# Gate projections placed behind head pairs in the first attention, and key halves copied by VectorE in the second

## The chip, the cores and the metric

One Trainium2 chip, one core. The metric is the device time of the whole kernel in microseconds (us), the median of three timed runs. Engines are named as in the profile: PE (TensorE matmuls), PEld (its weight loads), ACT (ScalarE), DVE (VectorE), POOL (GpSimd), SP (SyncE, which issues most transfers).

## What is computed

Two transformer blocks in a row on 512 tokens of width 1024, in float32. The parts that the change touches, shortened:

```python
# first block: window attention over latent and context keys, 16 query heads, 4 key heads
att_lat = window_ctx_attention(q_l, k_l, v_l, k_c, v_c, sink)
out_lat = merge_branches(p_lat, ssd_lat, att_lat, w_o_ssd, w_o_att, w_out)

def merge_branches(p, y_ssd, y_att, w_o_ssd, w_o_att, w_out):
    gates = jax.nn.sigmoid(p[..., G0:D_IN])
    g_ssd, g_att = gates[..., :D_MODEL], gates[..., D_MODEL:]
    return (g_ssd * (y_ssd @ w_o_ssd) + g_att * (y_att @ w_o_att)) @ w_out

# second block: forgetting attention, 12 heads of 64, one key head for each
s = jnp.einsum('bhqd,bhkd->bhqk', qi, kh)
s = s + Fi[..., None] - F[:, :, None, :]
s = jnp.where(key_pos[None, :] <= qpos[:, None], s, NEG)
p = jax.nn.softmax(s, axis=-1)
return jnp.einsum('bhqk,bhkd->bhqd', p, vh)
```

Around them stand a state-space branch (SSD), a feed-forward network with a convolution, an S5 branch, an attention over a memory, and the projections of all of them.

## The kernel before

All operands lie feature-major: 128 features on the partitions, 512 tokens along the free dimension. A projection multiplies eight 128x128 weight blocks with eight activation tiles. To keep float32 accuracy each operand is held as a rounded part (`hi`) and a remainder (`lo`), and `mm3` (L220) makes three matmuls of 128x512 for each block: hi x hi (L221), hi x lo (L222), lo x hi (L223). So a projection is 24 such matmuls.

`load_w` (L212) brings one block row of weights: an SP transfer of 512 KB into `raw` (3 buffers), the rounding `whi` on ACT (L181 through the helper `act`), the remainder `wlo` on DVE (L184 through the helper `tt`). `whi` and `wlo` have two buffers each, so two sets of weights can be ready at a time.

The order of each engine's instructions is made when the program is built. A planner goes through the instructions with a simulated clock and puts each on its engine's queue by priority, which is the order of the program text unless `tc.high_priority` raises it; a tile gets a buffer when one of its tag is free. `tc.issue_after(ins)` makes the instructions traced inside it, those on the engine of `ins`, stand behind `ins` in that engine's queue. On the chip each queue then runs in its fixed order, with semaphores between engines.

First attention (L714 to L921): eight head pairs i = 0 to 7, each 128 features of queries. `att_q(i)` (L831) projects the queries (two banks of PSUM for projections, `set_banks(2)`, L717), copies them to `u` (one buffer, shared with the gates' `tg`), rotates them (`roped`, partly on POOL) and splits them into `qq` (two buffers). `att(i)` (L839) works on two half pairs, the query blocks (0, 1) and (3, 2): for each head the scores (L852 to L856), row maxima on DVE (L782), exponentials on ACT, the scaling on DVE (L797), transposes on PE (L807, tile `pT`) and their copies on ACT (`pt`), and at the end of the half the product with the values (L872, tile `y`, 36 matmuls). The results go to `yaa` (pairs 0 to 3) and `yab` (pairs 4 to 7).

Work that does not hang on the attention is written between the pairs. `gate_ssd(m)` (L893), m = 0 to 7, projects one block of the SSD gates, takes a tanh (`tg`) and multiplies it into `p1`. `half_proj` (L881, tile `po`) multiplies `yaa` with half of `w_o_att`: each of its four steps needs all four tiles of `yaa` for two output blocks. `mod_steps(4, ...)` makes a modulation vector. In the text, gates stand behind the pairs by a list (L905): behind pair 1 gate 0, behind pair 2 gate 1, and so on, gates 5 and 6 behind pair 6, gate 7 behind pair 7; `half_proj` and `mod_steps` advance one step behind each of the pairs 4 to 7.

Second attention (L1560 to L1614): six head pairs, then four heads of the memory attention. `fox_in(i)` (L1560) projects the keys to `kk`, rounds them to `kh` and takes the remainder `kl`, then does the same with the queries. `fox(i)` (L1576) makes scores from `kh`, `kl`, `qq` and `lh` (L1590 to L1592; `lh` is partly cast on POOL, L1583), then the same chain of row maxima, exponentials, transposes and value products. `fox_in` of the next pair is written ahead of `fox` of this one. For head j of a pair, the rounded keys `kh[:, j]` fill all 128 partitions: the 64 of the head itself and a second copy in the other 64. Before, ACT makes both from `kk` (L1569), four 64x512 instructions for each pair.

Of the kernel before, what the change touches and what calls it, by code (L numbers as in the profile page):

```python
# [156 lines left out]
def emit(ctx, tc, A, out):  # L157
# [681 lines left out]
    def att(i):  # L839
# [4 lines left out]
        def score(n, hh):  # L844
# [11 lines left out]
                    T.matmul(sc[:, pos[j]:pos[j] + P], lhsT=identb, rhs=m_, start=False, stop=x == len(mk) - 1)  # L856
            return sc[:, rng[0]:rng[1]]

        for ns in ((0, 1), (3, 2)):
            pts = {}  # L860
            for hh in range(2):
                pr = softmax_rows([lambda n=n: score(n, hh) for n in ns], col("sink", 2 * i + hh), qp, 640, 4)
                for x, n in enumerate(ns):
                    nb = 5 if n in (1, 2) else 4
                    pts[n, hh] = transposed([pr[x][:, c * P:(c + 1) * P] for c in range(nb)], qp, 5, 4)

            with tc.high_priority(offset=1000):
                for n in ns[::-1]:
                    kbs = [0, 1] + [2 + j for j in (n - 1, n, n + 1) if 0 <= j < 4]
                    for x, kb in reversed(list(enumerate(kbs))):  # L870
                        for hh in (1, 0):
                            mm = T.matmul(py[64 * hh:64 * hh + 64, n * P:(n + 1) * P],  # L872
                                          lhsT=vx[:, kb, kv * 64:kv * 64 + 64], rhs=pts[n, hh][:, x],
                                          start=(x == len(kbs) - 1), stop=(x == 0)).ins
                            in_order(mm, first=(n == ns[1] and x == len(kbs) - 1 and hh == 1))
        ya = yaa if i < 4 else yab
        done = act(ya[:, 0, i % 4], py, AF.Copy)
        tt(ya[:, 1, i % 4], py, f(ya[:, 0, i % 4]), SUB)
        return done

    def half_proj(w, ya, consume):  # L881

# [19 lines left out]
    att_q(0)  # L902
    first = half_proj(A["w_oa"][0], yaa, lambda m, po: act(p2[:, m], po, AF.Copy))
    mod4 = mod_steps(4, mod_raw(4))
    fill = {1: [0], 2: [1], 3: [2], 4: [3], 5: [4], 6: [5, 6], 7: [7]}  # L905
    for i in range(8):
        if i < 7:
            att_q(i + 1)
        done = att(i)
        if i == 1:  # L910
            with tc.issue_after(done.ins):
                act(s5ls, s5ls, AF.Exp)
        for m in fill.get(i, []):
            gate_ssd(m)
        if i >= 4:
            next(first)
            next(mod4)
# [642 lines left out]
    def fox_in(i):  # L1560
# [4 lines left out]
        kl = kls[i % 2]  # L1565
        for j in range(2):
            src = kk[64 * j:64 * j + 64]
            for q0 in (0, 64):
                act(kh[q0:q0 + 64, j], src, AF.Copy)  # L1569
            tt(kl[64 * j:64 * j + 64, j], src, f(kh[64 * j:64 * j + 64, j]), SUB)  # L1570
        a = proj2(U_Q + i)
        r = rtile("r")
        act(r, a, AF.Copy, scale=0.125)
# [256 lines left out]
```

## Time and profile before

| what | us |
|---|---|
| median of three timed runs | 2050.18 |
| the three runs | 2053.67, 2044.92, 2050.18 |
| the profiled execution: its time | 2044.51 |
| the profiled execution: its span | 2042.7 |
| PE busy | 1967.9 (96%) |
| DVE busy | 1349.4 (66%) |
| ACT busy | 966.5 (47%) |

The span is the time from the first to the last instruction of the profiled execution; its own time is 1.8 us longer. Busy time of PE counts each matmul with its modelled latency, so that 96% doesn't mean that PE works at its peak, but a stretch in which its busy time is less than the stretch's length has idle time for certain. The granted clock is the share of TensorE's full clock in a stretch; 1.00 is 2.4 GHz, 0.50 is 1.2 GHz.

### The profile page before, as it was taken

The page shows a single profiled execution, that of the slowest core. Times are in us where ns is not written, and L with a number is a line of the kernel's source. Part 1 is how long each engine was busy: PE and PEld are TensorE (multiplying, and loading weights), DVE is VectorE, ACT ScalarE, POOL GpSimd, SP SyncE. Part 2 cuts the span into 40 slices and gives each one's busy share as a digit, 9 for nine tenths or more (in the row PEclk, how much of TensorE's full clock was granted, in tenths as well). Part 3 has the DMA queues.
Part 4 walks back from the last instruction along what each step waited for, and adds up shares of the span by engine and source line. Part 5 has one row for each costly group of instructions (what it writes and reads, how often), then busy time and mean ns, then how long its engine had stood idle before and what let it go on. Part 6 is the DMA issues. An engine that isn't in the chain of part 4 may idle for free.

```text
span 2042.7 us, 29489 instructions
## 1 busy us (share of the span) xinstructions
PE 1967.9 (96%) x11312; PEld 1614.0 (79%) x11312; DVE 1349.4 (66%) x2376; ACT 966.5 (47%) x1825; POOL 215.3 (11%) x358
## 2 busy tenths in 40 slices
PE   6998999999999899999999999999999899999998
PEld 4787888788888777778777778878988677888887
DVE  6878877878657775457988886673587655524344
ACT  6745554454235665435443244454465544423233
POOL 2111101101030000001001110001432100000000
PEclk9998999999999999999999999999999999999999
DMA  7444545545312023333354643335764112333332
GB/s 296 116 126 131 158 134 174 165 148 162 111 55 70 22 73 94 104 124 110 120 170 124 217 147 97 100 117 170 203 169 121 51 61 59 132 96 89 102 96 90
DMA packets 84667, 250.48 MB, mean 123 GB/s; under 512 B 11632, under 2 KB 23280, under 8 KB 83760
## 3 DMA queue, kind: packets, MB, share of 16 engines
q1 hardware_dynamic: 67376, 199.45, 31.4%
q0 software_dynamic: 17152, 49.17, 7.8%
q8 instruction: 89, 1.46, 0.3%
q14 instruction: 50, 0.41, 0.1%
HBM read 228.78 MB, written 16.65 MB: 120 GB/s over the span
## 4 chain that ended last, share of the span: by engine, by line
PE 81%; DVE 7%; issue 6%; ACT 3%; DMA 2%; POOL 1%; SPq 0%; DVEq 0%; ACTq 0%; POOLq 0%
PE p L221 6%; PE p L222 6%; PE p L223 6%; PE pl L221 5%; PE pl L223 5%; PE pl L222 5%; PE pT L807 2%; PE po L221 2%; PE po L223 2%; PE po L222 2%; PE ub L223 2%; PE ua L223 2%; PE ub L221 2%; PE ub L222 2%; PE ua L221 2%
## 5 line engine op out<-in xcount | busy, mean ns | idle before, releaser
L184 DVE TENSOR_TENSOR wlo<-raw,whi 128x1024 fp32r<-128x1024 f32 (+3 forms) x283 | 329.0, 1164 | 297.4 <-ACT whi L181 287.1
L181 ACT ACTIVATE whi<-raw 128x1024 fp32r<-128x1024 f32 (+3 forms) x283 | 282.3, 999 | 441.0 <-PE p L222 139.1
L221 PE MATMUL pl<-hl,whi 128*128 128x512 f32 x528 | 212.2, 402 | 3.8 <-DVE cv L187 3.0
L223 PE MATMUL pl<-hl,wlo 128*128 128x512 f32 x528 | 209.5, 397 | 0.7 <-DVE wlo L184 0.7
L222 PE MATMUL pl<-hl,whi 128*128 128x512 f32 x528 | 209.6, 397 | 0.0
L221 PE MATMUL p<-h,whi 128*128 128x512 f32 x504 | 201.3, 401 | 1.9 <-ACT uf L181 0.8
L223 PE MATMUL p<-h,wlo 128*128 128x512 f32 x504 | 201.7, 401 | 1.1 <-DVE wlo L184 1.1
L222 PE MATMUL p<-h,whi 128*128 128x512 f32 x504 | 201.9, 401 | 0.0
L221 PEld LDWEIGHTS pl<-hl,whi 128*128 128x128 f32 x528 | 100.4, 190 | 23.6 <-DVE cv L187 3.2
L223 PEld LDWEIGHTS pl<-hl,wlo 128*128 128x128 f32 x528 | 100.1, 190 | 23.2 <-DVE wlo L184 2.4
L221 PEld LDWEIGHTS p<-h,whi 128*128 128x128 f32 x504 | 95.6, 190 | 25.0 <-ACT uf L181 1.2
L181 ACT ACTIVATE p<-s,nm 128x512 f32<-128x512 f32 (+4 forms) x128 | 80.1, 627 | 74.2 <-PE pT L807 35.0
L223 PEld LDWEIGHTS p<-h,wlo 128*128 128x128 f32 x504 | 95.5, 189 | 23.3 <-DVE wlo L184 2.0
L782 DVE TENSOR_REDUCE nm<-s 128x1 f32<-128x512 f32 (+4 forms) x128 | 76.7, 611 | 55.5 <-PE s L1592 29.9
L222 PEld LDWEIGHTS p<-h,whi 128*128 128x128 f32 x504 | 95.4, 189 | 21.9 <-DVE h L184 0.3
L222 PEld LDWEIGHTS pl<-hl,whi 128*128 128x128 f32 x528 | 100.4, 190 | 14.9
L181 ACT ACTIVATE inj<-cs_t,dwt 128x128 f32<-128x128 f32 x256 | 81.1, 391 | 45.0 <-DVE es L635 36.9
L181 ACT ACTIVATE pt<-pT 128x512 f32<-128x512 f32 (+1 forms) x152 | 70.6, 478 | 63.5 <-PE pT L807 52.9
L807 PE MATMUL pT<-cs_t,p 128*128 128x128 f32 x440 | 72.4, 278 | 9.9 <-ACT pt L181 9.6
L640 POOL DMA_DIRECT2D cf<-rows x64 | 34.7, 549 | 354.4 <-PE y L659 348.4
L223 PE MATMUL pdn<-uh,wlo 128*128 128x512 f32 x176 | 69.4, 395 | 1.0 <-DVE wlo L184 1.0
L223 PE MATMUL ua<-hf,wlo 128*128 128x512 f32 x176 | 69.4, 394 | 0.7 <-DVE wlo L184 0.7
(543 smaller groups left out, 4771.7 us busy)
## 6 DMA issues: line engine op xcount, KB each, us to landing
raw<-in_w_ta SPq DMA_DIRECT2D x66, 512.0 KB, 3.6
raw<-in_w_tb SPq DMA_DIRECT2D x63, 512.0 KB, 3.6
raw<-in_w_up SPq DMA_DIRECT2D x44, 512.0 KB, 3.7
es<-rows POOLq DMA_DIRECT2D x64, 256.0 KB, 5.8
cf<-rows POOLq DMA_DIRECT2D x64, 256.0 KB, 4.8
raw<-in_w_mod SPq DMA_DIRECT2D x32, 512.0 KB, 3.8
raw<-in_w_os SPq DMA_DIRECT2D x16, 512.0 KB, 4.1
raw<-in_w_out SPq DMA_DIRECT2D x16, 512.0 KB, 3.6
```

The costliest lines, as they stand in the source:

```text
L181: return S.activation(o, i, f, **kw)
L184: return eng.tensor_tensor(o, a, b, op=op)
L221: T.matmul(ps, lhsT=wh, rhs=ah, start=first, stop=False)
L222: T.matmul(ps, lhsT=wh, rhs=al, start=False, stop=False)
L223: T.matmul(ps, lhsT=wl, rhs=ah, start=False, stop=last)
L640: QS.dma_start(out=c_, in_=rows[r, 1].partition_broadcast(P))
L782: V.tensor_reduce(nm[:, j:j + 1], src, axis=AX.X, op=MAX)
L807: T.transpose(pt[:, j * P:(j + 1) * P], b, ident)
```

## The change

First attention: the list of gates is replaced. Each entry now has a half: a gate with half 1 is traced behind the last value product (`y`) of the first half of pair i, a gate with half 0 behind the last value product of pair i - 1. `att` returns these two instructions. The instruction given to `issue_after` is a matmul, so that the gates' matmuls are tied, and their transfers, roundings and products on other engines are not. Second attention: ACT rounds only the head's own half of the keys, and DVE copies that rounded half to the other 64 partitions.

```diff
+        mids = []
         for ns in ((0, 1), (3, 2)):
...
+            mids.append(mm)
...
-        return done
+        return done, mids
...
-    fill = {1: [0], 2: [1], 3: [2], 4: [3], 5: [4], 6: [5, 6], 7: [7]}
+
+    fill = {0: [(1, 0)], 1: [(1, 1)], 2: [(0, 2), (1, 3)], 3: [(0, 4), (1, 5)], 5: [(1, 6)], 7: [(0, 7)]}
+    last_y = None
     for i in range(8):
         if i < 7:
             att_q(i + 1)
-        done = att(i)
+        done, mids = att(i)
...
-        for m in fill.get(i, []):
-            gate_ssd(m)
+        for half, m in fill.get(i, []):
+            after_ = mids[0] if half else last_y
+            with tc.issue_after(after_):
+                gate_ssd(m)
+        last_y = mids[1]
...
         for j in range(2):
             src = kk[64 * j:64 * j + 64]
-            for q0 in (0, 64):
-                act(kh[q0:q0 + 64, j], src, AF.Copy)
-            tt(kl[64 * j:64 * j + 64, j], src, f(kh[64 * j:64 * j + 64, j]), SUB)
+            own, other = slice(64 * j, 64 * j + 64), slice(64 - 64 * j, 128 - 64 * j)
+            act(kh[own, j], src, AF.Copy)
+            V.tensor_copy(kh[other, j], f(kh[own, j]))
+            tt(kl[own, j], src, f(kh[own, j]), SUB)
```

## Rows read from the trace of the kernel before

**Rows 1.** The page, part 1: busy us, share of the span, instructions.

```profile
PE 1967.9 (96%) x11312; PEld 1614.0 (79%) x11312; DVE 1349.4 (66%) x2376; ACT 966.5 (47%) x1825; POOL 215.3 (11%) x358
```

**Rows 2.** Busy us by stretch: length, PE, PEld, DVE, ACT, POOL, clock, DMA share, GB/s.

```profile
613.00:661.20 48.20, 48.20 (x309) 39.39 (x309) 35.63 (x72) 28.87 (x59) 2.56 (x2) 1.00 0.24 73
661.20:685.00 23.80, 22.80 (x185) 18.66 (x185) 17.11 (x38) 16.45 (x38) 1.28 (x1) 1.00 0.15 46
685.00:704.40 19.40, 15.95 (x150) 12.66 (x148) 14.63 (x35) 13.71 (x35) 1.28 (x1) 1.00 0.01 2
704.40:724.00 19.60, 16.62 (x155) 13.04 (x155) 13.87 (x36) 13.62 (x35) 0.00 (x0) 1.00 0.00 1
...
724.00:823.30 99.30, 99.23 (x743) 78.84 (x742) 61.89 (x133) 59.00 (x132) 2.55 (x2) 1.00 0.30 91
...
823.30:838.80 15.50, 12.49 (x129) 10.26 (x129) 7.40 (x18) 9.49 (x22) 0.00 (x0) 1.00 0.11 35
```

**Rows 3.** The same for instructions on `pl`, the projections: PE, PEld, DVE, ACT.

```profile
613.00:661.20 48.20, 35.13 (x135) 24.25 (x134) 0.00 (x0) 2.92 (x5) 1.00 0.24 73
...
704.40:724.00 19.60, 0.00 (x0) 0.00 (x0) 0.00 (x0) 0.00 (x0) 1.00 0.00 1
```

**Rows 4.** PE in order of time, first attention: start us, us, engine, line, instruction.

```profile
673.70 0.50 PE L221 MATMUL pl<-hl,whi 128*128 128x512 f32 x1
...
679.68 0.48 PE L221 MATMUL po<-yaa,whi 128*128 128x512 f32 x1
...
727.46 0.40 PE L223 MATMUL po<-yaa,wlo 128*128 128x512 f32 x1
...
731.07 0.50 PE L221 MATMUL pl<-hl,whi 128*128 128x512 f32 x1
```

**Rows 5.** Groups by shape, 1480 to 1700 us, ACT and DVE: count, busy us, mean ns.

```profile
L181 ACT ACTIVATE whi<-raw 128x1024 fp32r<-128x1024 f32 x23 | 24.3, 1057 | 22.1 <-PE p L222 10.2 <-issue 8.5 <-PE pg L222 3.3
L181 ACT ACTIVATE kh<-kk 64x512 fp32r<-64x512 f32 x20 | 12.6, 628 | 1.1 <-PE s L1590 0.8
...
L184 DVE TENSOR_TENSOR wlo<-raw,whi 128x1024 fp32r<-128x1024 f32 x22 | 26.8, 1220 | 5.1 <-ACT whi L181 4.6 <-DMA w<-s5k 0.3
L184 DVE TENSOR_TENSOR qq<-r,qq 64x512 fp32r<-64x512 f32 x10 | 6.9, 686 | 1.1 <-ACT qq L181 0.8
```

**Rows 6.** Instructions of tiles `fhi` and `lh`: duration ns min/median/max, first and last start.

```profile
L1544 DVE CAST fhi<-fe x1: 428/428/428, 1422.4 to 1422.4; 128x512 fp32r<-128x512 f32 x1
...
L1583 POOL CAST lh<-qq x12: 611/846/1602, 1475.6 to 1652.4; 64x512 fp32r<-64x512 f32 x12
```

**Rows 7.** ACT in order of time, second attention: start us, us, instruction.

```profile
1586.68 2.55 ACT L181 ACTIVATE kh<-kk 64x512 fp32r<-64x512 f32 x4
1589.25 1.06 ACT L181 ACTIVATE whi<-raw 128x1024 fp32r<-128x1024 f32 x1
1590.21 0.26 ACT L181 ACTIVATE pt<-pT 128x128 f32<-128x128 f32 x1
```

**Rows 8.** PE in order of time; in brackets the idle time before, and who ended it.

```profile
1590.53 0.74 PE L807 MATMUL pT<-cs_t,p 128*128 128x128 f32 x4 [2.78 <-ACT pt L181]
...
1621.09 0.66 PE L807 MATMUL pT<-cs_t,p 128*128 128x128 f32 x4 [2.55 <-ACT pt L181]
...
1691.89 0.66 PE L807 MATMUL pT<-cs_t,p 128*128 128x128 f32 x4 [1.36 <-ACT pt L181]
```

**Rows 9.** Busy us by stretch of the second attention, columns as in rows 2.

```profile
1585.00:1592.00 7.00, 4.22 (x24) 2.96 (x22) 4.36 (x11) 6.20 (x15) 2.29 (x4) 0.93 0.19 25
1592.00:1616.00 24.00, 23.18 (x137) 18.62 (x137) 18.54 (x40) 13.66 (x30) 1.32 (x1) 0.95 0.21 61
1616.00:1623.00 7.00, 4.45 (x25) 3.17 (x24) 3.95 (x9) 6.64 (x16) 0.84 (x1) 0.91 0.00 0
1623.00:1640.00 17.00, 15.86 (x97) 12.94 (x99) 9.81 (x23) 6.76 (x15) 0.85 (x1) 0.94 0.24 66
1640.00:1705.00 65.00, 61.26 (x365) 48.64 (x361) 32.42 (x79) 27.46 (x67) 0.85 (x1) 1.00 0.21 67
```

## The prediction

> **What bounds the kernel now.** I read the page's busy shares first: TensorE (PE) is busy 96% of the span and no other engine passes 66% [rows 1]. So a change counts only if it takes away idle time of PE (or time at its lower clock); PE's own work is the same before and after. Then I looked for that idle time stage by stage.
>
> In the first attention the busy time by head pair [rows 2] shows where it lies (length minus PE busy): none in pair 0, 1.00 us in pair 1, 3.45 in pair 2, 2.98 in pair 3, 0.07 in pairs 4 to 6 together, 3.01 in pair 7. The matmuls of the projections alone [rows 3] say why: about 135 of them, over five projections of 24, run beside pair 0, and none beside pair 3. An attention pair needs scores, row maxima, exponentials, transposes, so PE waits for ScalarE (ACT) and VectorE (DVE) unless it has other matmuls. The order of PE in that stretch [rows 4] names the blocker: a gate projection (gate 3, by the tanh that follows) starts at 673.7, the next to take its place is `po` of `half_proj`, at 679.7, and its last part runs only at 727.5, because its k=3 needs head pair 3. There are two projection banks (`set_banks(2)`). Two `po` sit in both from about 700 on, and the next projection starts at 731.1. The gates 0 to 3 had been spent early, where PE was full anyway.
>
> In the second attention the ACT queue [rows 7] shows four `kh` copies, 2.55 us in a row, then a weight rounding, and behind them the small `pt` copy at 1590.21 that PE's next transposes wait for. PE's gap there is 2.78 us, and in the same place one pair later 2.55 us [rows 8]. Both have a second cost: the granted clock falls to its lower level (1.2 instead of 2.4 GHz) for a while after each. Summing length times missing clock over the four stretches [rows 9]: 7 x 0.07 + 24 x 0.05 + 7 x 0.09 + 17 x 0.06 = 3.3 us.
>
> **First attention, step by step.** Nothing is added or removed; eight `gate_ssd` move. Their PE instructions are queued behind the last `y` matmul of a half pair: gate 0 in the middle of pair 0, gate 1 in the middle of pair 1, gate 2 at the end of pair 1, gate 3 in the middle of pair 2, gate 4 at its end, gate 5 in the middle of pair 3, gate 6 in the middle of pair 5, gate 7 at the end of pair 6. A projection is under 6.0 us of PE, transposes between included (673.7 to 679.7 [rows 4]); a starved half pair lacks (3.45 + 2.98) / 4 = 1.6 us. So one projection per half fills it more than three times over; it costs PE nothing new, as the same matmuls are taken from pair 0. And the `po` of `half_proj` now comes after gate 5 in program order, so it gets its weights, and so a bank, only in pair 3.
> What goes: 1.00 + 3.45 + 2.98 = 7.4 us in pairs 1 to 3, and half of pair 7's 3.0 (gate 7 fills the first half only): together 8.9 us.
> What comes: (a) the first half of pair 0 has only query projection 2 beside it. It is at least a starved half, 1.6 us, and at most a starved pair doubled, 6.4 us; I take two starved halves, 3.2, since nothing of that half is begun beforehand. (b) The pin holds only PE instructions. The gates' loads, roundings (ACT) and remainders (DVE) still come early and keep one of the two `whi`/`wlo` pairs each until the gate has run. Behind the parked weights stand the next projection's rounding and remainder, 1.06 + 1.22 = 2.3 us [rows 5]. The first such handover, between projections 1 and 2, has little cover: 0 to 1.9 us, I take 0.5. (c) Later handovers lie beside attention work; bounds 0 and 4 us, I take 1.0, which is less than one starved half, in pair 6, whose second half may be left without a projection.
> What is hidden: the tanh, the `p1` products and their POOL multiply are the same instructions; p1 is next read after the stage, so their lateness costs nothing, unless gate 7's lands at the very end, where the next projections cover it. On SP the gates' weight loads change their turn with the others' (0.5 MB each); DMA share is at most 0.30 in every stretch here [rows 2], so I cost them at nothing.
> Sum: -8.9 + 3.2 + 0.5 + 1.0 = -4.2 us; bounds -7.3 and +3.4.
>
> **Second attention, step by step.** Off ACT: 12 copies of 64x512 at 0.628 us = 7.5 us [rows 5]. Onto DVE: 12 copies. The trace has no such copy across partition halves. The nearest rows are a rounding of 128x512 on DVE, 0.428 us [rows 6], and a subtraction of 64x512 that does cross, 0.686 [rows 5]; I take 0.43, as the copy too has one input, so 5.2 us in all, at most 8.2. In four of the six `fox_in` other work covers the ACT block, and its relief is worth nothing. In the two of [rows 8] the block shrinks by two copies, 1.26 us each. The gaps that are left, about 1.5 and 1.3 us, are like the 1.36 us gap at 1691.9 [rows 8], in a stretch whose clock stayed at 1.00 [rows 9]. I take it that the clock stays up here too, and the 3.3 us come back. That is 2.5 + 3.3 = 5.8 us if the queues keep their order. They are planned anew, so I count one event whole and the other half: 4.4 us. Bounds: 8.7 (both gaps and the clock: 2.78 + 2.55 + 3.3) and, below nothing, -1.7 (four added copies of 0.43 in front of a row maximum that PE waits for).
> The change adds one wait: the DVE copy waits for its own half's ACT rounding. Behind it on DVE stand the `kl` remainder, which waited for the same thing before, then row maxima and weight remainders, for which PE and ACT wait. ACT is then free 1.26 us sooner, so the wait is short.
>
> **A rule against it.** The casts of `lh` on POOL take 0.61 to 1.60 us, the same work each time [rows 6]. The Trainium skill (SBUF — State Buffer, section "SBUF: two separate sides") says that DVE and GpSimd share one port pair by an exclusive lock, which a DVE copy in a two-port mode holds for its whole length. By that rule the four copies near the two gaps could hold up the casts 1.7 us, and the second part would give 2.7 instead of 4.4, the whole 6.9.
>
> **Sum.** -4.2 - 4.4 = -8.6 us. The profiled run took 2044.51 us (span 2042.7 and 1.8 around it), so 2035.9, a ratio of 0.9958. The median of the three timed runs lies 5.7 us above the profiled run; on it the ratio gives 2041.5.
>
> **Rivals.** Forecast: about 2041.5, between 2036 and 2047 (0.38).
> Both in full: the order holds and the first half of pair 0 is only a starved half: -7.3 - 8.7 = -16.0, 2034 (0.20). For it: the gaps are few and have one cause each. Against: the plan is new.
> Nothing comes of it: the planner fills the first attention a half early or late and gives the 4 us back elsewhere, and a weight rounding of 1.06 us takes the place of the `kh` copies in front of `pt`: 2050 (0.20). For it: 1.06 us of `whi` already stands in that block [rows 7].
> The DVE copies cost: they go ahead of row maxima or hold up the `lh` casts; the second part gives 1 us or less, whole sum -5.2, 2045 (0.12).
> Slower: parked gate weights starve PE. Each parked gate leaves one weight pair to all other projections; where a handover's 2.3 us isn't covered, a half without a gap becomes a starved one. It decides when more than about six of the ten halves of pairs 0, 1, 4, 5, 6 lose their cover (6 x 1.6 = 9.6 against 8.9 won). With all ten, and one fall of the clock as after the long gaps (3.3 / 2 = 1.7): 10 x 1.6 + 1.7 - 8.9 = +8.8 us, 2059, more if the second part loses too (0.10).
>
> **Chances.** A measurement of this kernel tells about 0.5%, 10.3 us, from no change. Faster by more: all of the full case and under half of the forecast, 0.37. Slower by more: over half of the starving case, 0.06. Within: 0.57. The range takes in the forecast, the full case with 3 us of scatter and nothing at all: 2031 to 2055; left out are the starving case and some of the full one's lower end.
>
> **What would show it.** In the trace after: PE idle of pairs 2 and 3 under 1 us each, with a projection beside each half; `po` not before pair 3; a gap of 2 to 4 us in the first half of pair 0; two `kh` copies in a row on ACT instead of four; PE gaps near 1590 and 1620 at 1.5 us or less with the clock at 1.00. I am wrong if projections bunch again, if PE idles in pairs 4 to 6, or if the long gaps stay with something else ahead of `pt`.

## The result and the profile after

| | before | after |
|---|---|---|
| median, us | 2048.89 | 2084.51 |
| its runs, us | 2044.92 to 2053.67 | 2081.98 to 2088.30 |
| profiled execution: time, span | 2044.51, 2042.7 | 2081.98, 2080.2 |

The ratio of after to before is 1.0162, with a 95% interval of 1.0141 to 1.0183: the change makes the kernel slower, by about 33 us (the two medians lie 35.6 apart). The prediction was 2041.5, its range ended at 2055, and slower had a chance of 0.06.

Five stretches tell where the 37.5 us of the two spans lie. The marks between them are instructions that both kernels have: the last `kx` copy on ACT (the first attention begins), the last `y` copy of the first attention, the first `kh` copy, and the last score matmul on `kh`.

| stretch | before, us | after, us | more |
|---|---|---|---|
| up to the first attention | 588.6 | 591.3 | 2.7 |
| first attention | 250.2 | 277.8 | 27.6 |
| between the attentions | 627.9 | 631.0 | 3.1 |
| second attention | 220.8 | 224.6 | 3.8 |
| rest | 355.2 | 355.5 | 0.3 |

No edit of the change touches the stretch between the attentions. In the ten kernels of this study whose matmuls stand there in the very order of before (before among them) it took 627.9 to 634.5 us. So its 3.1 us are scatter, which a sum over one profiled execution doesn't see. The first attention took 250.0 to 251.8 us in each of the nine kernels without ties (before among them), so its 27.6 us are no scatter.

The page after, part 1, answers to [rows 1]. PE is busy 18 us longer with the same 11312 matmuls, which is already a hint of a lower clock:

```profile
PE 1986.0 (95%) x11312; PEld 1624.1 (78%) x11312; DVE 1352.7 (65%) x2388; ACT 959.1 (46%) x1813; POOL 214.7 (10%) x358
```

Busy us by head pair of the first attention after, columns as in [rows 2], to which it answers; the limits are the ends of the pairs:

```profile
591.30:650.70 59.40, 50.62 (x323) 41.26 (x322) 30.92 (x57) 26.98 (x55) 4.94 (x3) 0.91 0.15 45
650.70:683.30 32.60, 27.65 (x197) 22.93 (x197) 19.53 (x43) 16.86 (x39) 1.27 (x1) 0.90 0.11 33
683.30:721.30 38.00, 35.24 (x225) 29.03 (x226) 22.77 (x50) 19.75 (x46) 1.34 (x1) 0.91 0.18 56
721.30:756.70 35.40, 33.80 (x233) 27.43 (x231) 22.93 (x50) 19.57 (x44) 2.14 (x1) 1.00 0.15 46
756.70:784.70 28.00, 24.93 (x219) 18.61 (x219) 18.86 (x42) 17.39 (x40) 1.27 (x1) 1.00 0.38 122
784.70:817.50 32.80, 29.40 (x223) 23.03 (x224) 18.62 (x46) 19.10 (x47) 0.00 (x0) 1.00 0.13 42
817.50:845.40 27.90, 26.77 (x210) 20.93 (x211) 16.55 (x35) 16.60 (x38) 2.19 (x1) 1.00 0.31 95
845.40:869.10 23.70, 22.20 (x177) 18.53 (x174) 11.32 (x26) 13.07 (x29) 0.00 (x0) 1.00 0.16 46
```

Length minus PE busy is idle time: 8.8, 5.0, 2.8, 1.6, 3.1, 3.4, 1.1 and 1.5, together 27.2 us, where before had 10.9 within the same marks. And the clock, 1.00 in every stretch of [rows 2], is 0.91, 0.90 and 0.91 in the first three pairs: 59.4 x 0.09 + 32.6 x 0.10 + 38.0 x 0.09 = 12.0 us lost to it. 16.3 of idle and 12.0 of clock make 28.3, a little more than the 27.6 us: of the 23.8 us at the lower clock PE is idle for 5.5, and these count in both.

The projections' matmuls alone (tile `pl`: PE, PEld, DVE, ACT), in the two halves of pair 0 and the first of pair 1, which answers to [rows 3]:

```profile
613.00:634.00 21.00, 0.00 (x0) 0.00 (x0) 0.00 (x0) 0.00 (x0) 0.76 0.08 26
634.00:650.70 16.70, 12.03 (x48) 8.64 (x48) 0.00 (x0) 1.16 (x2) 1.00 0.11 33
650.70:667.20 16.50, 0.00 (x0) 0.00 (x0) 0.00 (x0) 0.00 (x0) 0.79 0.11 33
```

There is no projection at all beside the two first halves, two in the second half of pair 0. PE's waits in the first attention after (who waits, for whom, us in total, times, longest) say the same: it waits for exponentials, and hardly for the projections' weights. One wait of 2.4 us is for a transfer of the modulation's weights, in pair 4; before has no such wait.

```profile
PE s L852 <- ACT p L181: 17.0, 16, 4.8
...
PE mod L320 <- DMA raw<-in_w_mod: 2.4, 1, 2.4
...
PE pl L223 <- DVE wlo L184: 0.4, 1, 0.4
```

The next two fences show why that is not for want of weights. First ACT and DVE in order of time (start us, us, instruction): the weights of query projection 2 are rounded at 611.42, as soon as projection 1 has freed them, and their remainder is made at 612.51.

```profile
611.42 1.06 ACT L181 ACTIVATE whi<-raw 128x1024 fp32r<-128x1024 f32 x1
612.51 1.23 DVE L184 TENSOR_TENSOR wlo<-raw,whi 128x1024 fp32r<-128x1024 f32 x1 [0.33 <-ACT whi L181]
```

Then PE, which answers to [rows 4], and behind it on ACT the two evictions that tell whose projections these were (`tg` is a gate's, `u` a query's):

```profile
618.00 0.80 PE L852 MATMUL s<-kx,qq 128*128 128x512 f32 x1 [4.84 <-ACT p L181]
622.04 0.58 PE L852 MATMUL s<-kx,qq 128*128 128x256 f32 x1 [1.27 <-ACT p L181]
...
634.76 0.48 PE L221 MATMUL pl<-hl,whi 128*128 128x512 f32 x1
...
641.41 0.58 ACT L181 ACTIVATE tg<-pl 128x512 f32<-128x512 f32 x1
647.95 0.58 ACT L181 ACTIVATE u<-pl 128x512 f32<-128x512 f32 x1
```

PE stands idle 4.84 us for the exponentials of the first half, then 1.27, and only behind the half's value product do projections come: gate 0, then query projection 2, whose weights had been ready since 613.7. Gate 0 is tied there; projection 2 is not, but it stands behind gate 0 in the text.

In the second attention the new instructions took what was expected of them (groups by shape, count, busy us, mean ns, answering to [rows 5]):

```profile
L1577 DVE CAST kh<-kh 64x512 fp32r<-64x512 f32 x12 | 5.1, 422 | 0.7 <-ACT kh L181 0.5
...
L181 ACT ACTIVATE kh<-kk 64x512 fp32r<-64x512 f32 x12 | 7.5, 628 | 0.4 <-PE s L1598 0.2
```

The gaps of [rows 8] are gone, and others are there instead, with a stretch of low clock behind them that answers to [rows 9]:

```profile
1620.24 0.38 PE L1598 MATMUL s<-kh,qq 128*128 128x256 f32 x1 [1.50 <-ACT p L181]
...
1622.19 0.66 PE L807 MATMUL pT<-cs_t,p 128*128 128x128 f32 x4 [1.14 <-ACT pt L181]
```

```profile
1623.00:1635.00 12.00, 12.00 (x52) 10.65 (x53) 9.03 (x23) 6.61 (x17) 3.31 (x7) 0.57 0.24 55
```

12 x 0.43 = 5.2 us are lost there, against 3.3 in all of [rows 9]. (Kernels that keep the order of before in the second attention lost 1.7 to 5.1 us there, so this part alone is no sign of the change.)

### The profile page after: what moved, and what is told of

The parts are those of the page before. It is cut to its first block, busy times and chain, and to the rows that moved or that the text cites. A ratio compares the mean times of both kernels' runs of the same rounds, so it can differ in the third digit from the quotient of the medians.

```text
span 2080.2 us, 29501 instructions
## 1 busy us (share of the span) xinstructions
PE 1986.0 (95%) x11312; PEld 1624.1 (78%) x11312; DVE 1352.7 (65%) x2388; ACT 959.1 (46%) x1813; POOL 214.7 (10%) x358
## 5 line engine op out<-in xcount | busy, mean ns | idle before, releaser
L221 PEld LDWEIGHTS p<-h,whi 128*128 128x128 f32 x504 | 95.2, 189 | 26.1 <-ACT kk L181 1.4
L807 PEld LDWEIGHTS pT<-cs_t,p 128*128 128x128 f32 x440 | 53.8, 146 | 22.3 <-ACT pt L181 9.6
```

The lines of the kernel that those rows point to most:

```text
L221: T.matmul(ps, lhsT=wh, rhs=ah, start=first, stop=False)
L807: T.transpose(pt[:, j * P:(j + 1) * P], b, ident)
```

## The experiments

Theory H: the untied query projections stand in line behind the tied gate that precedes them in the text; the half that should have had them is bare, PE idles there, and the clock falls behind the gaps. Its rivals: the key copies cost the time (K), the ties or the gates' parked weights starve PE wherever they are (P, W). For the second part: VectorE's copies cost by themselves (C), or the order that comes out decides (M).

The runs in one table. In both attentions "lost" is PE's idle time plus, summed over thirty slices, the length times what the clock lacks to 1.00; before has 10.9 + 0.0 and 8.7 + 3.4, after 27.2 + 11.9 and 9.7 + 5.1.

| kernel | median, us | ratio to before, 95% interval | first attention: length, lost | second: length, lost |
|---|---|---|---|---|
| ties only | 2080.9 | 1.0149 (1.0132 to 1.0167) | 279.5, 26.1 + 15.4 | 219.6, 9.0 + 1.7 |
| ties, own bank | 2059.3 | 1.0047 (1.0030 to 1.0063) | 261.1, 17.1 + 3.4 | 220.4, 8.7 + 3.4 |
| own bank behind projection 1 | 2060.7 | 1.0049 (1.0035 to 1.0064) | 260.6, 16.0 + 5.1 | 219.7, 9.0 + 1.8 |
| ties, own weight buffers | 2072.5 | 1.0116 (1.0090 to 1.0142) | 273.7, 24.9 + 6.8 | 215.0, 8.1 + 3.4 |
| no ties | 2050.2 | 1.0007 (0.9997 to 1.0017) | 250.0, 7.2 + 1.7 | 220.8, 8.9 + 3.4 |
| one tie | 2056.3 | 1.0029 (1.0012 to 1.0047) | 257.2, 12.2 + 5.1 | 222.3, 8.7 + 5.1 |
| all halves filled | 2065.8 | 1.0077 (1.0057 to 1.0097) | 266.4, 21.5 + 3.4 | 219.1, 8.7 + 1.7 |
| keys only | 2062.0 | 1.0058 (1.0041 to 1.0076) | 250.2, 10.9 + 0.0 | 230.2, 10.1 + 10.2 |
| keys, subtract first | 2056.1 | 1.0030 (1.0015 to 1.0045) | 250.2, 10.9 + 0.0 | 226.6, 8.4 + 8.5 |
| no key copies | 2043.7 | 0.9972 (0.9958 to 0.9986) | 251.8, 10.9 + 1.8 | 216.0, 4.0 + 1.7 |
| both copies | 2049.9 | 0.9998 (0.9984 to 1.0013) | 250.3, 10.9 + 0.0 | 221.1, 9.0 + 3.4 |
| first head's copies | 2052.3 | 1.0011 (0.9997 to 1.0025) | 251.8, 10.9 + 1.7 | 221.0, 8.3 + 3.4 |
| second head's copies | 2048.5 | 0.9993 (0.9981 to 1.0006) | 251.8, 10.9 + 1.8 | 218.5, 7.6 + 1.7 |
| copies on GpSimd | 2047.1 | 0.9981 (0.9966 to 0.9995) | 250.2, 10.9 + 0.0 | 215.9, 6.4 + 0.0 |

Length minus lost is 238 to 242 us in every first attention. In the second it is 208 to 210, but for the kernel with own weight buffers (203.5; its buffers are parted in the whole kernel, and there 3.2 us more stand behind that stretch). So the work of PE is the same everywhere, and what the edits move is idle time and clock.

How far these two repeat can be read from kernels that share an order. Own bank, one tie and all halves filled run the second attention in the order of before (but for a few matmuls in own bank): its idle time is 8.7 us in all four, and the clock takes 1.7 to 5.1. The seven kernels that differ from before in the keys alone have its order in the first attention: 10.9 of idle each, and 0 or 1.7 to 1.8 of clock. After and ties only share their order there, on all engines: 27.2 and 26.1 of idle, 11.9 and 15.4 of clock. So the idle time belongs to the order, and the clock's part scatters by up to 3.5 us with the order unchanged.

**Each half alone.** Ties only: after with the old key copies.

```diff
-            act(kh[own, j], src, AF.Copy)
-            V.tensor_copy(kh[other, j], f(kh[own, j]))
-            tt(kl[own, j], src, f(kh[own, j]), SUB)
+            for q0 in (0, 64):
+                act(kh[q0:q0 + 64, j], src, AF.Copy)
+            tt(kl[64 * j:64 * j + 64, j], src, f(kh[64 * j:64 * j + 64, j]), SUB)
```

> Only the first half of the change: the new list and the eight ties, with the key copies on ScalarE as before. Theory H (the untied query projections stand in line behind the tied gate that precedes them in the text, so pair 0's first half and pair 5's first half are bare and the clock halves in the gaps): it carries nearly all of the loss, 2049 + 28 to 31 = 2077 to 2080 us, the first attention ends 27 to 31 us later against its start than before, and its matmul order and its half-clock stretches are those of the changed kernel. Rival K (the key copies on VectorE are what costs): 2049 to 2056 us here.

Keys only: before with the same lines the other way round.

> Only the second half of the change: the kernel before with the other half's keys copied by VectorE from the rounded half. Theory H: within 5 us of the kernel before, 2044 to 2054 us, and nearest to 2051 (the second attention of the changed kernel was 3.9 us longer, some 2 of it a slower clock in a stretch where the plan came out otherwise); the first attention is unchanged. My prediction's own step said 4.4 us less, 2044.5. Rival K: 2070 or more.

Ties only lost 31 us, keys only 12, both together 33 to 36. So the ties carry nearly the whole loss of the change, as theory H had it. Keys only lost more than H said (2062 against 2044 to 2054) and far less than K; that it costs 12 alone and some 3 beside the ties is a question of its own, taken up below.

**Is it the line, and what makes it?** The list alone, without the ties:

```diff
-            with tc.issue_after(after_):
-                gate_ssd(m)
+            gate_ssd(m)
```

> The new list without the ties: the gates stand in the text where e1 has them, nothing holds them back. Theory H: the projections run as soon as their weights and a bank are there, as in the kernel before, nothing stands in line behind a held gate until the output projection's first half does: 2045 to 2058 us. Rival L (the new list alone, by which gates and query projections are planned in another order, costs the time, and the ties nothing): 2070 to 2080.

2050.2: the new order of the text costs nothing, the ties do. Next, the ties stay, and the two projection banks of PSUM are parted, one for the queries and one for the gates (from pair 4 on, one for the modulation row):

```diff
+        if sep[0]:
+            tag = "dg" if name == "mod" or (sep[0] == 1 and not kind[0]) else "dq"
+            return banks["p"].tile([P, 512], F32, tag=tag, name=name, bufs=1)
         return banks["p"].tile([P, 512], F32, tag="d", name=name, bufs=banks["n"])
...
     def att_q(i):
+        kind[0] = 1
         a = proj(T_Q + i, False)
+        kind[0] = 0
...
```

> The ties of e1 with one thing more: in the first attention the two projection banks of PSUM are no longer shared in turn, one is for the query projections and one for the gates (from pair 4 on one for the fourth modulation row and one for all else). Theory H, with the bank as what makes the line: query projection 2 runs beside pair 0's first half and the later ones pass the gates, so pairs 0 to 3 have a projection in every half; 20 to 35 us less than e1, that is 2043 to 2058 us, and no half-clock stretch beside pairs 0 to 3. Rival P (it is the tied gates' weights that hold up the following loads, or the ties starve TensorE wherever they are): within 8 us of e1, 2070 to 2080.

And the counterpart: banks shared as before, but of the two pairs of weight buffers one is for the queries and one for all else.

```diff
-        hi, lo = to or (wp.tile([P, 1024], F32R, tag="w" + nm, name="w" + nm, bufs=2) for nm in ("hi", "lo"))
+        hi, lo = to or (wp.tile([P, 1024], F32R, tag="w" + nm + str(slot()), name="w" + nm, bufs=1) for nm in ("hi", "lo"))
...
```

> The ties of e1 with the two split weight buffers parted instead of the banks: one pair for the query projections, one for gates and output projection; the two PSUM banks are shared in turn as in e1. Theory H with the bank as the line: no gain, within 5 us of e1's 2081, 2074 to 2086, the query projections still behind the gates. Rival W (the gates' parked weights hold up the query projections): 2050 to 2062, as the kernel with parted banks or better.

Parted banks bring back 21.6 of the 31.6 us between ties only and before. The projections' matmuls of that kernel in the two halves of pair 0 and the first of pair 1 (columns as above) stand where after had none:

```profile
613.00:634.00 21.00, 6.00 (x24) 4.35 (x24) 0.00 (x0) 0.15 (x1) 0.84 0.17 51
634.00:648.10 14.10, 7.66 (x31) 5.56 (x32) 0.00 (x0) 1.18 (x2) 1.00 0.12 39
648.10:662.30 14.20, 4.71 (x19) 3.10 (x17) 0.00 (x0) 0.00 (x0) 1.00 0.09 26
```

The whole of query projection 2 (24 matmuls) runs beside pair 0's first half. With parted weights and shared banks it doesn't; the ten matmuls of the first row here are gate 0's and begin at 630.78, behind the half's value product:

```profile
612.00:634.00 22.00, 2.59 (x10) 1.91 (x11) 0.00 (x0) 0.00 (x0) 0.77 0.07 25
...
638.18 0.58 ACT L182 ACTIVATE tg<-pl 128x512 f32<-128x512 f32 x1
644.25 0.58 ACT L182 ACTIVATE u<-pl 128x512 f32<-128x512 f32 x1
```

The gate is again evicted first (638.18) and the query projection behind it (644.25), and the first attention is still 23.5 us longer than before. The total, 2072.5, lies a little under what H expected (2074 to 2086), and 10 us over the rival's upper end; of the 8.5 us that it gains on ties only, 5.8 lie in the first attention, and why is not shown. There parted banks gain 18.4. So the line in which the matmuls stand forms mainly at the shared bank. That the planner hands out buffers of one tag in the order of the text, though projection 2's own bank was free, is the likely reason; it is inferred, not shown.

One shared place is left that no run parts: the one buffer of `u` and `tg`. In the kernel with own banks the matmuls of query projection 2 end at 620, but its copy to `u` comes 25 us later, released by the product that reads gate 0's `tg` (ACT, then DVE):

```profile
643.00 0.58 ACT L182 ACTIVATE tg<-pl 128x512 f32<-128x512 f32 x1
645.72 0.60 ACT L182 ACTIVATE u<-pl 128x512 f32<-128x512 f32 x1 [1.32 <-DVE p L188]
...
645.01 0.68 DVE L188 SCALAR_TENSOR_TENSOR p<-tg,p 128x512 f32<-128x512 f32 x1
```

Until then projection 2 holds the one bank of the queries. How much of the 10 us that parted banks don't bring back hangs on this line is open.

**What one bare half costs.** One tie put back into the list without ties, that of gate 0:

```diff
-            gate_ssd(m)
+            with tc.issue_after(mids[0]) if m == 0 else ExitStack():
+                gate_ssd(m)
```

> The list without ties (2050 us) with one tie put back, that of gate 0 behind pair 0's first half. Theory H: the one tie takes the projections out of pair 0's first half, TensorE stands idle there for some 8 us and its clock halves behind the gaps for some 10 us (5 us lost), as in the changed kernel; the work comes later beside pairs that were bare, which gives some of it back: 2054 to 2065 us, the half-clock stretch of 10 us beside pair 0 and no such beside pairs 1 to 3. Rival N (it takes many ties to cost anything): within 4 us of the list without ties.

2056.3, within what H expected; by the time alone the rival isn't excluded, as its upper end, 2054, lies inside the interval. What decides is the trace: PE has the two gaps of after again, to the hundredth:

```profile
616.97 0.80 PE L852 MATMUL s<-kx,qq 128*128 128x512 f32 x1 [4.84 <-ACT p L181]
...
621.01 0.58 PE L852 MATMUL s<-kx,qq 128*128 128x256 f32 x1 [1.27 <-ACT p L181]
```

Pair 0 has 8.8 us of idle time, and 5.1 us go to the clock; the projections that it doesn't get fill other halves, so that 7.2 us of these 13.9 are left in the stretch, against no ties.

**What is left with parted banks.** In that kernel projection 0 waits 1.30 us for an eviction of the values (`vx`) and projection 1 waits 1.41 us for that of projection 0 (`u`). Parting the banks one step later takes both away:

```diff
-    set_banks(2)
-    sep[0] = 1
     att_q(0)
...
         if i < 7:
             att_q(i + 1)
+        if i == 0:
+            set_banks(2)
+            sep[0] = 1
```

> The kernel with a bank of its own for the query projections (2059 us), but the banks are parted only behind query projection 1, so that projections 0 and 1 don't wait for each other's eviction (there the two waits of 1.30 and 1.41 us). Theory H with the bank as the line: 2.5 to 3 us less, 2055 to 2058, and what is left against the kernel before is pair 0's first half (query projection 2 runs ahead of it, not through it: 3.1 us idle and 7 us at half clock) and the bare halves behind pair 4. Rival: no change, 2058 to 2062, because the softmax of pair 0 waits for projection 1 in either.

No gain: 2060.7, as the rival said, though not quite for its reason. Both waits are gone, but projection 2 now runs earlier against the softmax of pair 0, the gap there is 3.38 instead of 2.25 us, and the clock takes 5.1 instead of 3.4 (a difference within its scatter):

```profile
590.70:648.60 57.90, 52.12 (x329) 42.73 (x328) 32.83 (x63) 28.87 (x59) 4.98 (x3) 0.91 0.18 55
```

Then a list by which, with parted banks, pair 0's first half has two projections and every later half up to pair 3 has one:

```diff
-    fill = {0: [(1, 0)], 1: [(1, 1)], 2: [(0, 2), (1, 3)], 3: [(0, 4), (1, 5)], 5: [(1, 6)], 7: [(0, 7)]}
+    fill = {0: [(2, 0), (1, 1)], 1: [(1, 2)], 2: [(1, 3)], 3: [(1, 4)], 4: [(2, 5)], 5: [(1, 6)], 6: [(1, 7)]}
...
-            after_ = mids[0] if half else last_y
-            with tc.issue_after(after_):
+            after_ = {0: last_y, 1: mids[0], 2: None}[half]
+            with tc.issue_after(after_) if after_ else ExitStack():
...
```

> The kernel with banks of their own for query projections and gates, with another list: gate 0 untied, so that pair 0's first half has two projections, and one tied gate for each later half up to pair 3, gate 5 untied beside pair 4, gates 6 and 7 tied to pairs 5 and 6. Theory H (a tie is free, and gains, where a projection is there for every half and none stands in line behind it): the first attention's idle and slow-clock time falls from 10.9 us in the kernel before to 3 to 7 us, 2041 to 2048 us. Rival P (ties cost by themselves): 2055 or more.

This refutes what I still held of the change's idea. 2065.8 is 16 us slower than before, in the range of the rival by which ties cost by themselves, and the first attention loses 24.9 us, not 3 to 7. PE's waits in it (engine, line, who ended the wait, us in total, times, longest):

```profile
PE s L858 <- ACT p L182: 5.7, 5, 2.8
PE mod L324 <- DMA raw<-in_w_mod: 3.8, 3, 1.7
PE pT L811 <- ACT pt L182: 3.5, 12, 0.6
...
```

and pairs 0 to 5 of it, and behind them the projections' matmuls (tile `pl`) in the first half of pair 5:

```profile
587.50:646.20 58.70, 53.82 (x345) 44.24 (x344) 33.22 (x63) 29.71 (x59) 4.57 (x3) 0.97 0.20 63
646.20:673.50 27.30, 26.00 (x197) 21.06 (x198) 19.13 (x43) 17.14 (x41) 1.36 (x2) 1.00 0.13 40
673.50:700.70 27.20, 25.90 (x197) 20.96 (x198) 19.02 (x43) 17.20 (x41) 1.26 (x2) 1.00 0.12 39
700.70:730.20 29.50, 27.48 (x216) 21.80 (x217) 20.29 (x47) 17.60 (x41) 1.62 (x2) 1.00 0.19 56
730.20:765.20 35.00, 32.95 (x242) 26.09 (x241) 21.25 (x44) 18.95 (x45) 1.27 (x1) 1.00 0.26 84
765.20:800.10 34.90, 29.17 (x214) 23.35 (x215) 20.82 (x49) 19.54 (x48) 0.00 (x0) 0.95 0.12 38
...
763.70:780.00 16.30, 0.00 (x0) 0.00 (x0) 0.00 (x0) 0.00 (x0) 0.90 0.10 36
```

Pairs 1 to 3, where each half has a projection, still idle 1.3, 1.3 and 2.0 us, mostly in small waits for `pt` and `p`. That is 4.6 together against 7.4 in before: the fill wins there, but little. The loss lies where the projections were taken from. Pair 0 idles 4.9 against 0.4; it has two projections behind projections 0 and 1, where before had over four. Pairs 4 to 6 idle 2.1, 5.7 and 2.2 us against 0.1 together. Of that, 5.3 lie in the first half of pair 5, which is bare in spite of the list, and 3.8 in this attention are late loads of the modulation's weights. So this run doesn't have every half filled, and it has parted banks as well: neither the price of a tie by itself nor that of a thin spread by itself is shown by it.

**The keys.** Leave out the copies, so that ACT's relief stands alone, or let both engines make them, so that DVE's load stands alone. The cuts are against the loop of keys only, that of both copies against before. The kernel without the copies sets the other half of the key tiles to zero once, on GpSimd, ahead of the attention; its scores are not those of the reference.

```diff
             act(kh[own, j], src, AF.Copy)
-            V.tensor_copy(kh[other, j], f(kh[own, j]))
             tt(kl[own, j], src, f(kh[own, j]), SUB)
...
```

> The kernel before without the 12 copies of keys into the other half: no engine makes them (that half of the tiles stays at zero, so the second attention's numbers are wrong), which takes 12 x 0.63 = 7.5 us off ScalarE and adds nothing to VectorE. Theory C (VectorE's 12 copies of 0.42 us, in front of its softmax work, are what made the keys-only kernel 12 us slower): 2049 or less, about 2045 by the sum of my prediction. Theory M (the keys ready earlier make the plan come out otherwise, small matmuls of the state space layer meet the waits of the first head pairs, and TensorE's clock halves there): the loss can stay although there is less work, 2050 to 2062, with half-clock stretches in the second attention longer than the 6.8 us of before.

```diff
             for q0 in (0, 64):
                 act(kh[q0:q0 + 64, j], src, AF.Copy)
+            V.tensor_copy(kh[64 - 64 * j:128 - 64 * j, j], f(kh[64 * j:64 * j + 64, j]))
```

> The kernel before with VectorE's 12 copies of keys made as well, over ScalarE's, which stay (the same values; the scores wait for the last of them). It prices VectorE's copies without the relief of ScalarE. Theory C: the relief was worth 5.7 us and keys-only lost 12, so the copies alone cost 10 to 18 us: 2060 to 2067. Theory M: 2046 to 2062, and as much of the difference as there is more half-clock time in the second attention.

ACT's relief alone is worth 6 us (2043.7), as theory C had it; M, which allowed a loss, missed. VectorE's copies alone cost nothing (2049.9, ratio 0.9998, to within 3 us), where theory C, by the difference of relief and keys only, had said 10 to 18 us. They took the same time as in after:

```profile
L1570 DVE CAST kh<-kh x12: 420/422/425, 1472.8 to 1624.9; 64x512 fp32r<-64x512 f32 x12
```

C falls with that in its turn. A gain of 6 and a price of nothing make a loss of 12 when they are put together, so the sum of the parts is the wrong way to count. What the trace of keys only shows in its costliest place, DVE, ACT and PE together:

```profile
1595.31 1.45 DVE L187 SCALAR_TENSOR_TENSOR yv<-uf,cols,yp 128x512 f32<-128x512 f32 x1 [1.75 <-DMA yp<-yb]
1596.79 0.63 ACT L181 ACTIVATE t<-yv 128x512 f32<-128x512 f32 x1 [0.84 <-DVE yv L187]
1597.33 0.46 ACT L181 ACTIVATE p<-s,nm 128x256 f32<-128x256 f32 x1
1597.93 0.39 PE L1591 MATMUL s<-kh,qq 128*128 128x256 f32 x1 [2.45 <-ACT p L181]
...
1601.17 0.42 DVE L1570 CAST kh<-kh 64x512 fp32r<-64x512 f32 x1
```

PE waits 2.45 us for an exponential; on ACT that stands behind `t` of the S5 branch, which waits for `yv` on DVE, which waited 1.75 us for a transfer. The key copy comes 3 us after the gap: it isn't in the chain, as far back as the transfer; what made that late isn't shown. Behind the gap the clock is at its lower level for most of 16 us, in a stretch of small S5 matmuls:

```profile
1600.00:1616.00 16.00, 15.98 (x65) 13.91 (x66) 10.06 (x25) 6.96 (x17) 4.67 (x9) 0.57 0.25 49
```

Of the 9.4 us that the second attention got longer here, 1.4 are idle time and 6.8 clock. The 10.2 us of clock lie outside the 1.7 to 5.1 that the order of before has.

Three kernels try whether it goes by the copies or by the order that comes out. The same copies with two lines exchanged:

```diff
-            V.tensor_copy(kh[other, j], f(kh[own, j]))
             tt(kl[own, j], src, f(kh[own, j]), SUB)
+            V.tensor_copy(kh[other, j], f(kh[own, j]))
```

> The keys-only kernel with two lines exchanged: VectorE makes the remainder kl before it makes the copy, so that the same work is planned a little otherwise. Theory C: the same 12 copies cost the same, 2059 to 2065. Theory M: the time goes with the half-clock stretches that this plan happens to meet, 2046 to 2066, and the difference to the keys-only kernel is that of those stretches, at half of their length.

And half of the copies, for the first head of each pair or for the second (here the first):

```diff
-            V.tensor_copy(kh[other, j], f(kh[own, j]))
+            if j == 0:
+                V.tensor_copy(kh[other, j], f(kh[own, j]))
+            else:
+                act(kh[other, j], src, AF.Copy)
```

> The kernel before with VectorE making the other half's copy for the first head of each pair only: 6 copies move from ScalarE, 6 stay. Its instruction order in the second attention is far from that of the kernel before, about as far as that of keys-only. Theory C2 (the time goes by how many copies move): half of keys-only's loss, 2054 to 2058. Theory M (it goes by the order that comes out, through TensorE's waits and half-clock stretches): 2046 to 2062, and not the same as its twin with the second head's copies, though the work is the same.

> The twin: VectorE makes the copy for the second head of each pair only, again 6 of 12. Its order is near that of the kernel before. Theory C2: 2054 to 2058, as its twin. Theory M: within 4 us of the kernel before or faster by up to 3 (half the 5.7 us that ScalarE's relief was worth), 2046 to 2052, with no more half-clock time in the second attention than before.

Subtract first loses 6 us where keys only lost 12, with the same work; of the 3.6 us between their second attentions 1.7 are clock, which scatters by as much, and 1.7 idle time. The twins with six copies come out at 2052.3 and 2048.5, neither to be told from before. The number of copies would give 2054 to 2058; the second lies below that, the interval of the first reaches to 2055. What speaks against the number is rather that the same twelve copies went with a loss of 0 (both copies), 6 and 12 us. Whether the twins differ from each other is open: their intervals overlap. Last, the copies on GpSimd, with the remainder first:

```diff
             act(kh[own, j], src, AF.Copy)
-            V.tensor_copy(kh[other, j], f(kh[own, j]))
             tt(kl[own, j], src, f(kh[own, j]), SUB)
+            G.tensor_copy(kh[other, j], f(kh[own, j]))
```

> The kernel before with the other half's keys copied from the rounded half by GpSimd (and the remainder kl made ahead of it). ScalarE is relieved of its 12 copies as in the kernel without copies, which was 5.7 us faster. Theory C (it is VectorE's extra work, between the softmax's own steps, that ate the gain and more): GpSimd has little else there, the gain stays, 2042 to 2048 us. Theory M (any new plan of this stretch meets the clock's fall): 2050 to 2062. Theory G, a third: GpSimd's casts of this shape took 0.6 to 1.6 us in the profile of before, so the keys come later than ScalarE's second copy and the scores wait, 2050 to 2056 without more half-clock time than before.

2047.1, ratio 0.9981 (0.9966 to 0.9995): about half of the relief stays, though GpSimd's copies take up to five times as long as VectorE's. That lies in theory C's range (2042 to 2048). M, by which any new order of this stretch meets the clock's fall, missed here a second time, and so did G, by which late keys make the scores wait.

```profile
L184 DVE TENSOR_TENSOR kl<-kk,kh x12: 673/707/1121, 1468.8 to 1618.5; 64x512 fp32r<-64x512 f32 x12
...
L1571 POOL CAST kh<-kh x12: 609/960/2173, 1468.9 to 1618.7; 64x512 fp32r<-64x512 f32 x12
```

Its second attention has no time at the lower clock, but the profiled execution (2041.2) is one of its fastest, 6 us under the median, and shows the good case. It is the one version with the reference's work that beat both kernels, by 0.05 to 0.34% of the time before; with fourteen kernels compared, so narrow a margin may be chance.

Neither theory stands as I stated it. Shown is that VectorE's 12 copies cost nothing by themselves, to within 3 us, that the loss doesn't go by their number alone, and that PE's work is 208 to 210 us in all these kernels with 5.7 to 20.3 us of idle time and low clock around it. That the order which the planner makes of copies and relief together brings the loss is an inference from that and from the chain above, which holds no key copy. No run has the moved copies in the order of before, so this stays open.

## Why the prediction was wrong, step by step

**What bounds the kernel** held: PE's work at full clock was the same in all runs, and every difference is idle time or clock.

**Step (a), "the first half of pair 0 has only query projection 2 beside it": this is the step that failed.** It didn't have even that. I read from the text that the tie holds gate 0's matmuls and nothing else. It also holds the untied projection that comes after it in the text and shares its banks (own bank: 21.6 us back; own weights: the gate still first). The same line had been before my eyes: in [rows 4] the projections wait behind `po`, which itself waits. I named that blocker, moved it, and didn't ask what would stand at the head of the line next. It is the tied gate, in pairs 0 and 1 and again in pair 5; their first halves have no projection and idle 8.7, 5.0 and 3.3 us.

**The size of (a)** was off as well. With projection 2 in its place, pair 0 idles 5.4 us more than before and loses 5.1 to the clock (own bank behind projection 1: 5.8 of idle, 0.4 before), 10.5 against my 3.2 and my bound of 6.4. I took the price of a bare half, 1.6, from pairs 2 and 3 of before. Pair 0's gap in after is 4.84 us, where the longest in a bare half of before was this (PE in order of time):

```profile
718.40 0.39 PE L852 MATMUL s<-kx,qq 128*128 128x256 f32 x1 [1.28 <-ACT p L181]
```

That pair 0 has no half ahead of it, as I had noted, can't be the whole reason: the bare first half of pair 1, which has one, idles 5.0 us with a gap of 2.66. Why these cost so much more than the bare halves of before is open.

**The clock** was in my sum for the second attention alone. In the first it took 12.0 of the 27.6 us. Every row of [rows 2] said 1.00, and I carried that over to an order with gaps of up to 4.84 us.

**"One projection per half fills it more than three times over"** failed too. Counting matmul time against idle time, 6 us against 1.6, says nothing of when the waits come. In after the first half of pair 2 has its projection, 24 matmuls of gate 2, and still idles 2.6 us, with the clock at 0.82:

```profile
683.30:701.70 18.40, 15.83 (x101) 13.18 (x101) 13.91 (x33) 11.30 (x27) 0.00 (x0) 0.82 0.17 57
```

With one in each half, 1.3 and 2.0 us are left in pairs 2 and 3 (all halves filled). Nor were the projections free to take away: pairs 4 to 6, which had idled 0.1 us together, idle 7.6 after. So the 8.9 us that were to go did not: pairs 1 to 3 idle 9.3 us after, against 7.4 before. Only pair 7 did as the sum had it (1.5 left of 3.0).

**Steps (b) and (c), the handovers of weights,** were small as I said: after has 0.4 us of waits for a remainder, and before has as much. The weight transfers, which I put at nothing, cost the one wait of 2.4 us for the modulation. So the slower rival, parked weights, gave the right sign by the wrong mechanism. Its price was far too low, because it counted only half pairs without cover at 1.6 us and one fall of the clock.

**Second attention, -4.4:** taken one by one, the copy took 0.422 us (0.43 predicted), ACT's relief is worth 6 us (5.8 in the sum), and the long gaps of [rows 8] went. That the relief's sum fits is partly luck: without the copies the idle time fell by 4.7 us, where I had 2.5, and the clock's part by 1.7, where I had 3.3. What failed is the clause "if the queues keep their order", and that I gave the other case half of a gain instead of a loss. The second attention got 3.8 us longer in after, 9.4 in keys only; my bound on that side was 1.7. Nothing of it goes to the rule weighed there. By the Trainium skill (SBUF — State Buffer, section "SBUF: two separate sides") GpSimd's casts could have been held up by VectorE's copies. With both copies made, the `lh` casts took 609 to 1197 ns, no longer than the 611 to 1602 of [rows 6], and the time was that of before. But in none of the six traces with copies on VectorE does one of them run at the same time as an `lh` cast: no run here shows that price, and none puts it to the test. Where the two engines did meet, with the key copies on GpSimd, they held each other up: VectorE's `kl` took up to 1.12 us beside such a copy, and 0.67 to 0.69 without one.

**The sum's base:** the profiled execution lay 5 us under the median, and I took the ratio over to the median. The stretch that nobody edited explains that by its own scatter of 627.9 to 634.5 us; it is small against the miss.

Of the signs that I named, "a gap of 2 to 4 us in the first half of pair 0" (4.84), "a projection beside each half" and "PE idle of pairs 2 and 3 under 1 us" (2.8 and 1.6) came out wrong, and so did the clock at 1.00 near the gaps of the second attention (0.57 behind gaps of 1.50 and 1.14 us). `po` not before pair 3 and two `kh` copies in a row came out right. The sign of being wrong, idle time in pairs 4 to 6, came true (7.6 us).

## What to carry to other kernels

Before an instruction is tied late, ask who takes the next buffer of the same tag behind it: an untied neighbour waits with it, and buffers of its own set most of it free. Filling work isn't free to move: one projection in a bare half took away less idle time than came back where it had stood, so price the place that it leaves as well as the place that it fills. And where a planner makes the order, the price of an edit isn't the sum of its instructions: a free copy and a gainful relief lost 12 us together, and 6 with two lines exchanged, so weigh the new order as a case of its own, with a loss in it.

## What the runs showed of the hardware

- The granted clock fell to its lower level behind gaps shorter than the 2.55 us of before: gaps of 1.50 and 1.14 us, 2 us apart, and then 0.57 over 12 us that begin with small matmuls (128x64) of the S5 branch. In the bare halves of before, with gaps up to 1.28 us, it stayed at 1.00 [rows 2], as it did behind the 1.36 of [rows 8]. In the first attention the same work lost 0 to 15.4 us to it in different orders; one and the same order lost 11.9 in one profile (after) and 15.4 in another (ties only).
- A copy of 64x512 from one partition half to the other took 0.422 us on DVE, 0.61 to 2.17 on GpSimd, 0.628 on ACT. Beside GpSimd's copies DVE's remainder `kl` took up to 1.12 us, where 0.69 was the longest in every kernel with no such copies.
